# The first convolution group's sums in two attention tiles instead of the fourth raw buffer, and transposes a step or two later

## The chip, the cores and the metric

The kernel runs on one core of a Trainium2 chip. The metric is the device time of one execution in microseconds (us), lower is better. PE is the matrix engine, ACT the scalar engine, DVE the vector engine, SP the engine whose queue issues the loads and most stores.

## The reference

One encoder layer on 256 tokens with 4096 channels. The stream is normalised, projected by one 4096 x 13312 matrix, and split into a convolution branch and an attention branch.

```python
h = layer_norm(x, emb_ln_g, emb_ln_b)
p = h @ w_in                       # c_b, c_c, c_h, c_z, a_q, a_k, a_v, a_z
y_conv = c_b * centred_short_conv(c_c * c_h, conv_w) * silu(c_z)
y_attn = banded_window_attention(a_q, a_k, a_v, sink) * silu(a_z)
y = concat([y_conv, y_attn]) @ w_out
out = layer_norm(2 ** 0.25 * h + y, ln_g, ln_b)
```

All arrays are float32. The convolution is over three neighbouring tokens.

## The kernel before

**Chunks and steps.** The input projection is cut into 26 chunks of 512 columns: K, V, then for each of four attention groups the gate chunk AZ and the query chunk Q, then for each of four convolution groups the chunks CC, CH, CZ, CB. A chunk is a list of steps, 302 in all. A step of kind "in" loads 1 MB of weights and makes 24 matmuls of 512 columns; "half" loads 512 KB and makes 12; "pair" loads 512 KB, forms sums of weight blocks on DVE (a seven-product scheme for a 2 x 2 block product) and makes 21 matmuls of 256 columns. From the fourth chunk on, all have the same twelve steps: in, pair, pair, half, pair, in, pair, pair, in, pair, pair, in. Below, offset n is the step n places behind the first of its chunk (0 to 11).

**The split.** Weights are float32 and the matmul takes a reduced type, so each raw piece is split into a high part (`split_hi`, ACT, L200, tile `whi`) and the rest (`split_lo`, DVE, L204, tile `wlo`). Both are made three steps ahead, and each has three buffers, so the high part of step j+3 can be written only when step j's matmuls are done.

**The raw buffers.** Raw pieces lie in `w0`, `w1`, `w2` and, while the list `extra` names them, in further ones: `w6` of the pool `pw`, later `w7` and `w8` of the pool `pc`. `loads(j)` gives the next piece the buffer whose last piece is oldest. With three buffers it may take the one whose piece is split in the current step (j+3), with more only one whose piece was split a step earlier:

```python
            if u > j + (2 if len(bs) > N_W else 3):
                break
```

All these loads stand in SP's queue in program order, so a load that waits for its buffer holds up those behind it, and stores as well.

**The order in a step.** The order on each engine is the program's: matmuls of step j, `split_hi(j + 3)`, the functions that `at(j, ...)` entered for this step, `loads(j)`, `sums(j + 4)` (L181 to L183, pairs only), `split_lo(j + 3)`. The functions in `later` are the rest of the layer: a chunk's pair products are joined (`pair_copy`, then `pair_sums` a step later), the chunk is completed five steps after its last pair (`whole`, L677), and heads are spread over some 30 steps by `SPREAD` (`scores`, `s_add`, `p_tr`, `p_lo`, `pv`, `out_z`).

**Memory around the change.** Attention tiles lie in the pool `pa`, among them one tile `z` and one tile `q` of 128 x 1024, and `zT`, whose products `out_z` stores to DRAM (`yd`). When attention is over, `open_pc` closes `pa` and opens `pc` in its place, with the convolution's tiles `tm`, `ug`, `t0`, `t1`, the buffers `w7`, `w8` and `yl`. The first convolution group's chunks CC and CH are computed while the last heads are still running, before `pc` exists. Their sums go side by side into the tile in `w6`, which is why `w6` leaves `extra` 18 steps before the chunk CZ of that group begins. That beginning is step `z0` = 134. `product` multiplies the one by the other in place (L682, at z0 + 6), `conv_tr` transposes the product on PE and scales it into `t` on ACT (L696, at z0 + 8 and + 9), `conv_mul` adds the two neighbours on DVE (L702, L704, at z0 + 9 and + 10). `open_pc` stands at z0 + 8. In the later groups, and for the gate chunk CB (`product`, `gate_tr`, `gate_mul`), the same functions stand in the chunk that follows: `product` at offset 4, the transposes at 5 and 6, the rest at 7 and 9.

For the gate chunk AZ, `z_act` applies the SiLU on ACT (L524) at offset 5 of the next chunk, and `z_tr` transposes the result on PE (L481) and copies it to `zT` (L529) at offsets 11 and 13, in the first group at 6 and 7. Transposes, scores and the products with V share two PSUM banks (`att`).

Of the kernel before, what the change touches and what calls it, by code (L numbers as in the profile page):

```python
# [8 lines left out]
F32 = mybir.dt.float32  # L9
F32R = mybir.dt.float32r  # L10
AF = mybir.ActivationFunctionType
ALU = mybir.AluOpType
AX = mybir.AxisListType

P = 128
# [17 lines left out]
W = 512  # L33
# [65 lines left out]
def encoder_kernel(ctx: ExitStack, tc: tile.TileContext, x, emb_g, emb_b, wi, ws, conv_w, sink, wo, ln_g, ln_b, out):  # L99
    nc = tc.nc  # L100
# [57 lines left out]
    def loads(j):  # L158

        nonlocal nxt  # L160
        while nxt < len(steps) and nxt <= j + 7:
            (u, _), bs = w_bufs(nxt)
            if u > j + (2 if len(bs) > N_W else 3):
                break
            load(nxt)
            nxt += 1
# [31 lines left out]
    def split_hi(j):  # L198
        wh[j] = half_tile(j, "whi")
        nc.scalar.activation(part(j, wh[j]), part(j, raw[j]), AF.Copy)  # L200

    def split_lo(j):
        wl[j] = half_tile(j, "wlo")
        nc.vector.tensor_tensor(part(j, wl[j]), part(j, raw[j]), part(j, wh[j]).bitcast(F32), op=ALU.subtract)  # L204
        raw.pop(j)
# [22 lines left out]
    def mm(j):  # L228
        _, ci, q = steps[j]
        hi, lo = wh.pop(j), wl.pop(j)  # L230
        first = j == 0 or steps[j - 1][1] != ci
        last = j == N_IN - 1 or steps[j + 1][1] != ci
        pk, k0 = (2, 2 * q) if steps[j][0] == "half" else (PK, q * PK)
        for k in range(pk):
            kt = k0 + k
            for i in range(2):
                if first and k == 0:
                    acc[ci, i] = ps_acc.tile([P, W], F32, name="acc")
                a = acc[ci, i]
                xh, xl = xT[:, kt, i * P:(i + 1) * P], xT[:, kt, S + i * P:S + (i + 1) * P]  # L240
                hk, lk = hi[:, k * W:(k + 1) * W], lo[:, k * W:(k + 1) * W]
                nc.tensor.matmul(a, xh, hk, start=(first and k == 0), stop=False)  # L242
                nc.tensor.matmul(a, xh, lk, start=False, stop=False)  # L243
                nc.tensor.matmul(a, xl, hk, start=False, stop=(last and k == PK - 1))  # L244
# [3 lines left out]
    def mm_pair(j):  # L248


        _, ci, p = steps[j]
        hi, lo = (t.pop(j).rearrange("p (b w) -> p b w", w=HW) for t in (wh, wl))
        last = p == npairs(ci) - 1
        if p == 0:
            for k in range(2):
                pacc[ci, k] = ps_p.tile([P, 2, HW], F32, name="pacc")
        a, b = 2 * p, 2 * p + 1
        x = lambda kt, i: (xT[:, kt, i * HT:(i + 1) * HT], xT[:, kt, (2 + i) * HT:(3 + i) * HT])
        sc = lambda n: (SC[p][:, 0, n, :], SC[p][:, 1, n, :])
        p0, p1, c0, c1 = pacc[ci, 0], pacc[ci, 1], acc[ci, 0], acc[ci, 1]  # L260
        for (ah, al), w, o, opens, closes in (
                (x(a, 0), 2, p0[:, 0, :], True, False), (x(b, 0), 3, c0[:, 0:HW], False, False),
                (sc(2), 1, c0[:, HW:W], False, False), (x(b, 1), 7, c1[:, 0:HW], False, False),
                (sc(0), 5, p1[:, 1, :], True, False), (x(a, 1) if ci < OUT else sc(3), 6, p0[:, 1, :], False, True),
                (sc(1), 4, p1[:, 0, :], False, True)):
            nc.tensor.matmul(o, ah, hi[:, w, :], start=(opens and p == 0), stop=False)  # L266
            nc.tensor.matmul(o, ah, lo[:, w, :], start=False, stop=False)  # L267
            nc.tensor.matmul(o, al, hi[:, w, :], start=False, stop=(closes and last))  # L268
# [186 lines left out]
    pw = phs.enter_context(tc.tile_pool(name="pw", bufs=1))  # L455
    extra.append((pw, "w6"))
    pa = ph.enter_context(tc.tile_pool(name="pa", bufs=1))
# [30 lines left out]
    st_ = {}  # L488
# [140 lines left out]
    def x_sums(p, t):  # L629

        x = xT[:, 2 * p:2 * p + 2, :]
        xf = t[:, 0:2 * S].rearrange("p (k t) -> p k t", k=2)
        nc.vector.tensor_tensor(xf, x[:, :, 0:S].bitcast(F32), x[:, :, S:2 * S].bitcast(F32), op=ALU.add)
        a11, a12, a21, a22 = (xf[:, k, i * HT:(i + 1) * HT] for i in range(2) for k in range(2))
        s = t[:, 2 * S:4 * S].rearrange("p (k t) -> p k t", k=4)
        for k, o0, o1, op in ((0, a21, a22, ALU.subtract), (3, s[:, 0, :], a11, ALU.subtract),
                              (1, a11, a21, ALU.subtract), (2, a12, s[:, 3, :], ALU.add)):
            nc.vector.tensor_tensor(s[:, k, :], o0, o1, op=op)
        if SC[p].shape[2] == 4:
            return halves(SC[p][:, 0, :, :], SC[p][:, 1, :, :], s)  # L640
        halves(SC[p][:, 0, :, :], SC[p][:, 1, :, :], s[:, 0:3, :])
        halves(x[:, 0, HT:2 * HT], x[:, 0, 3 * HT:4 * HT], s[:, 3, :])

    def sum_tile(ci):

        if ci >= OUT:
            return R[:, :, (ci - OUT) * W:(ci - OUT + 1) * W]
        kind = IN_ORDER[ci]
        if kind >= C_AZ:
            return pa.tile([P, 2, W], F32, name="z")  # L650
        if kind >= C_Q:
            return pa.tile([P, 2, W], F32, name="q")
        name = "ug" if kind < C_CC or C_CH <= kind < C_CZ else "tm"
        if pc is not None:
            return pc.tile([P, 2, W], F32, name=name)
        if name == "tm":
            st_["cu"] = pw.tile([P, 2, 2, W], F32, name="w6", bufs=1)
        return st_["cu"][:, 1 if name == "ug" else 0, :, :]

    def pair_copy(ci):  # L660
        e = st_["e", ci] = sum_tile(ci)
        nc.scalar.activation(e[:, 0, 0:HW], pacc[ci, 0][:, 0, :], AF.Copy)
# [15 lines left out]
        return t  # L678

    def product(key, other):  # L680
        u = st_[key]
        nc.vector.tensor_tensor(u, u, st_[other], op=ALU.mult)  # L682

    def end_cc(ci, c):
        st_["c"] = whole(ci)
# [61 lines left out]
    def at(j, fn, *a):  # L747
        later.setdefault(j, []).append((fn, a))
# [4 lines left out]
    def chunk_end(j, ci):  # L753
        c0, fn = next((c, f) for c, f in ENDS if IN_ORDER[ci] >= c)
        g = IN_ORDER[ci] - c0
        fn(ci, g)
        if fn is end_k:
            at(j + 1, k_turn, g)
        if fn is end_cz:
            at(j + 4, s_act)  # L760
        if fn is end_z:
            at(j + 5, z_act)
            for b in range(2):
                at(j + 11 + 2 * b, z_tr, g, b) if g else at(j + 6 + b, z_tr, g, b)
        if fn is end_q:
            h = g * GROUP
            for t, f, a in SPREAD:
                at(j + t, f, a if f in (q_tr, q_lo) else h + a)
            if g < 2:
                at(j + 22, k_load, g)  # L770
                at(j + 32, v_load, g)
        if fn in (end_ch, end_cb):
            key, other, tr, mul = ("u", "c", conv_tr, conv_mul) if fn is end_ch else ("g", "s", gate_tr, gate_mul)
            last = ci == len(IN_ORDER) - 1
            if last:
                product(key, other)
            else:
                at(j + (6 if ci == c_ch0 else 4), product, key, other)
            for t, f, b in ((2, tr, 0), (2, tr, 1), (3, mul, 0), (3, mul, 1)) if last else (
                    (8, tr, 0), (9, tr, 1), (9, mul, 0), (10, mul, 1)) if ci == c_ch0 else (  # L780
                            (5, tr, 0), (6, tr, 1), (7, mul, 0), (9, mul, 1)):
                at(j + t, f, g, b)

    c_ch0 = IN_ORDER.index(C_CH)
# [7 lines left out]
    z0 = next(j for j, u in enumerate(steps) if u[1] == c_ch0 + 1)  # L792
    for j in range(n_pro, N_IN):
        kind, ci, q = steps[j]
        if j == z0 - 18:
            extra.clear()
        if j == z0 + 10:
            extra.insert(0, (pw, "w6"))
        mm_pair(j) if kind == "pair" else mm(j)
        split_hi(j + 3)  # L800
        for fn, a in later.pop(j, []):
            fn(*a)
        if kind == "pair" and q == PAIRS[ci] - 1:
            pair_copy(ci)
            at(j + 1, pair_sums, ci)
        if j in X_SUMS:
            x_sums(X_SUMS.index(j), pa.tile([P, 4 * S], F32, name="xs", tag="zT", bufs=2))
        if steps[j + 1][1] != ci or j == N_IN - 1:
            if ci == c_ch0:
                at(j + 9, open_pc)  # L810
            if PAIRS[ci]:
                at(j + (4 if j < N_IN - 1 else 1), chunk_end, j + 1, ci)
            else:
                chunk_end(j, ci)
        loads(j)
        sums(j + 4)
        split_lo(j + 3)
# [180 lines left out]
    for n, (c0, w, pk, j0) in enumerate(chunks):  # L998
        us = out_units(n)
        np_ = sum(u[0] == "opair" for u in us)  # L1000
        for t, (kind, _, q) in enumerate(us):
            j = j0 + t
# [118 lines left out]
```

## Time and profile before

| | |
|---|---|
| time, median of 3 runs | 1547.57 us (1547.43 to 1549.18) |
| time of the profiled execution | 1548.43 us |
| its span, first to last instruction | 1546.7 us |
| PE busy | 1524.0 us, 99% |
| DVE busy | 1319.0 us, 85% |
| ACT busy | 777.6 us, 50% |
| DMA | 315.65 MB, mean 204 GB/s |
| TensorE clock granted | 1.00 of full speed |

A matmul's shown duration covers its pipeline; successive matmuls overlap, so PE's busy share is not the share of its peak. In a row of a group stand the count, the busy time, the mean duration in ns, and the idle time of the engine just before the group's instructions with what ended it. In a row of waits stand who waited, for whom, the sum in us, the number of times and the longest. In a row of the timeline stand the start and the duration in us, and in brackets the idle time before it and what ended that. The chain of waits follows the work that ended last back to its causes. SPq is SP's queue of DMA issues.

### The profile page before, as it was taken

The numbers are of one execution on the slowest core, as the hardware profiler recorded it, in microseconds if no ns is written. First come the engines' busy times: TensorE is split into PE (matmuls) and PEld (weight loads), VectorE is DVE, ScalarE is ACT, GpSimd is POOL, SyncE is SP. The second block draws the span as 40 slices with busy tenths as digits, with TensorE's granted clock in tenths as the row PEclk, the third lists the DMA queues.
The fourth block names the chain that finished last, engine by engine and source line by source line (L and its number), as shares of the span: only waits on it lengthen the run. The fifth ranks groups of instructions, "written<-read, shape, count | busy, mean of one in ns | idle before, by whom it ended". The sixth has DMA issues, their size and how long they took to land.

```text
span 1546.7 us, 21715 instructions
## 1 busy us (share of the span) xinstructions
PE 1524.0 (99%) x8843; PEld 1330.5 (86%) x8843; DVE 1319.0 (85%) x1535; ACT 777.6 (50%) x666; POOL 1.3 (0%) x7
## 2 busy tenths in 40 slices
PE   7999999999999999999999999999999999999998
PEld 4888889988988988788888888888888888888897
DVE  7769799899899898988898989998898688888656
ACT  5544546656565554544455455545555444443331
POOL 0000000000000000000000000000000000000000
PEclk9999999999999999999999999999999999999999
DMA  7545554555655545655555555556557756656654
GB/s 290 201 177 196 199 198 162 204 181 191 208 190 171 170 171 201 227 192 210 199 191 204 194 210 196 191 190 229 197 201 274 275 185 226 250 204 225 261 180 141
DMA packets 71428, 315.65 MB, mean 204 GB/s; under 512 B 8512, under 2 KB 12576, under 8 KB 50336
## 3 DMA queue, kind: packets, MB, share of 16 engines
q1 hardware_dynamic: 70320, 312.43, 56.7%
q10 hardware_dynamic: 1008, 1.84, 0.3%
q8 instruction: 69, 1.13, 0.3%
q14 instruction: 31, 0.25, 0.0%
HBM read 305.23 MB, written 8.91 MB: 203 GB/s over the span
## 4 chain that ended last, share of the span: by engine, by line
PE 84%; DVE 11%; DMA 2%; ACT 1%; issue 1%; SPq 0%; ACTq 0%; DVEq 0%
PE acc L242 12%; PE acc L243 12%; PE acc L244 12%; PE acc L908 6%; PE acc L910 6%; PE acc L909 6%; DVE wlo L204 5%; PE pacc L267 4%; PE pacc L266 4%; PE pacc L268 4%; PE acc L266 3%; PE acc L267 3%; PE acc L268 3%; DMA w<-in_ws 2%; DVE w L181 1%; ACT whi L200 1%
## 5 line engine op out<-in xcount | busy, mean ns | idle before, releaser
L200 ACT ACTIVATE whi<-w 128x2048 fp32r<-128x2048 f32 (+1 forms) x352 | 618.1, 1757 | 638.9 <-DVE w L183 209.2
L204 DVE TENSOR_TENSOR wlo<-w,whi 128x2048 fp32r<-128x2048 f32 (+1 forms) x352 | 733.0, 2085 | 147.2 <-ACT whi L200 146.8
L242 PE MATMUL acc<-whi,xT 128*128 128x512 f32 x988 | 390.8, 395 | 0.0
L243 PE MATMUL acc<-wlo,xT 128*128 128x512 f32 x988 | 387.9, 393 | 1.7 <-DVE wlo L204 1.7
L244 PE MATMUL acc<-whi,xT 128*128 128x512 f32 x988 | 387.5, 392 | 0.0
L244 PEld LDWEIGHTS acc<-whi,xT 128*128 128x128 f32 x988 | 185.8, 188 | 41.6
L243 PEld LDWEIGHTS acc<-wlo,xT 128*128 128x128 f32 x988 | 185.8, 188 | 40.8 <-DVE wlo L204 3.8
L242 PEld LDWEIGHTS acc<-whi,xT 128*128 128x128 f32 x988 | 185.8, 188 | 36.3
L908 PE MATMUL acc<-whi,xT 128*128 128x512 f32 (+1 forms) x496 | 182.8, 369 | 0.0
L910 PE MATMUL acc<-whi,xT 128*128 128x512 f32 (+1 forms) x496 | 181.7, 366 | 0.0
L909 PE MATMUL acc<-wlo,xT 128*128 128x512 f32 (+1 forms) x496 | 180.7, 364 | 0.5 <-DVE wlo L204 0.5
L181 DVE TENSOR_TENSOR w<-w 128x512 f32<-128x512 f32 x175 | 119.6, 683 | 8.9 <-DMA w<-in_ws 8.9
L910 PEld LDWEIGHTS acc<-whi,xT 128*128 128x128 f32 x496 | 93.1, 188 | 16.8
L909 PEld LDWEIGHTS acc<-wlo,xT 128*128 128x128 f32 x496 | 93.1, 188 | 16.1 <-DVE wlo L204 0.8
L908 PEld LDWEIGHTS acc<-whi,xT 128*128 128x128 f32 x496 | 93.2, 188 | 14.4 <-issue 0.4
L267 PE MATMUL acc<-wlo,xT 128*128 128x256 f32 x362 | 101.1, 279 | 0.0
L266 PE MATMUL acc<-whi,xT 128*128 128x256 f32 x362 | 101.0, 279 | 0.0
L268 PE MATMUL acc<-whi,xT 128*128 128x256 f32 x362 | 100.9, 279 | 0.0
L266 PE MATMUL pacc<-whi,xT 128*128 128x256 f32 x346 | 98.9, 286 | 0.1
L267 PE MATMUL pacc<-wlo,xT 128*128 128x256 f32 x346 | 96.8, 280 | 0.5 <-DVE wlo L204 0.5
L268 PE MATMUL pacc<-whi,xT 128*128 128x256 f32 x346 | 96.5, 279 | 0.0
L267 PE MATMUL pacc<-wlo,SC 128*128 128x256 f32 x330 | 93.1, 282 | 0.0
(236 smaller groups left out, 2019.1 us busy)
## 6 DMA issues: line engine op xcount, KB each, us to landing
w<-in_wi SPq DMA_DIRECT2D x112, 1024.0 KB
w<-in_ws SPq DMA_DIRECT2D x198, 512.0 KB
w<-in_wo SPq DMA_DIRECT2D x43, 1024.0 KB
R<-in_wo SPq DMA_DIRECT2D x13, 1024.0 KB
x<-in_x SPq DMA_DIRECT2D x7, 512.0 KB
yl<-yd SPq DMA_DIRECT2D x7, 512.0 KB
xc<-in_x SPq DMA_DIRECT2D x14, 256.0 KB
R<-in_ws SPq DMA_DIRECT2D x6, 512.0 KB
```

The costliest lines, as they stand in the source:

```text
L181: nc.vector.tensor_tensor(s01, b22, b12.to_broadcast([P, 2, HW]), op=ALU.add)
L200: nc.scalar.activation(part(j, wh[j]), part(j, raw[j]), AF.Copy)
L204: nc.vector.tensor_tensor(part(j, wl[j]), part(j, raw[j]), part(j, wh[j]).bitcast(F32), op=ALU.subtract)
L242: nc.tensor.matmul(a, xh, hk, start=(first and k == 0), stop=False)
L243: nc.tensor.matmul(a, xh, lk, start=False, stop=False)
L244: nc.tensor.matmul(a, xl, hk, start=False, stop=(last and k == PK - 1))
L266: nc.tensor.matmul(o, ah, hi[:, w, :], start=(opens and p == 0), stop=False)
L267: nc.tensor.matmul(o, ah, lo[:, w, :], start=False, stop=False)
L268: nc.tensor.matmul(o, al, hi[:, w, :], start=False, stop=(closes and last))
L908: nc.tensor.matmul(o, yh, hk, start=first, stop=False)
L909: nc.tensor.matmul(o, yh, lk, start=False, stop=False)
L910: nc.tensor.matmul(o, yl, hk, start=False, stop=last)
```

## The change

- `sum_tile`: while `pc` is not open, the sums of CC go to tile `z` and those of CH to tile `q`, both of `pa`.
- `product`: while `pc` is not open, the result goes to a new tile in `w6` (one half of it is used), no longer over its own operand. It moves from z0 + 6 to z0 + 8.
- `w6` stays a raw buffer until z0 + 4 (before: z0 - 18) and comes back at z0 + 12 (before: z0 + 10).
- `open_pc` moves from z0 + 8 to z0 + 9.
- In the first convolution group `conv_tr` moves from z0 + 8 and + 9 to + 10 and + 11, `conv_mul` from + 9 and + 10 to + 18 and + 21.
- In the other groups `conv_tr`, and in all groups but the last `gate_tr` (the same transposes for the chunk CB), move from offsets 5 and 6 to 6 and 7; their `product` (offset 4) and `conv_mul` or `gate_mul` (7 and 9) stay.
- `z_tr` of the first attention group moves from offsets 6 and 7 to 8 and 9.

```diff
-        if name == "tm":
-            st_["cu"] = pw.tile([P, 2, 2, W], F32, name="w6", bufs=1)
-        return st_["cu"][:, 1 if name == "ug" else 0, :, :]
+        return pa.tile([P, 2, W], F32, name="q" if name == "ug" else "z")
...
     def product(key, other):
-        u = st_[key]
-        nc.vector.tensor_tensor(u, u, st_[other], op=ALU.mult)
+        u, o = st_[key], st_[other]
+        if pc is None:
+            st_[key] = pw.tile([P, 2, 2, W], F32, name="w6", bufs=1)[:, 0, :, :]
+        nc.vector.tensor_tensor(st_[key], u, o, op=ALU.mult)
...
-                at(j + 11 + 2 * b, z_tr, g, b) if g else at(j + 6 + b, z_tr, g, b)
+                at(j + 11 + 2 * b, z_tr, g, b) if g else at(j + 8 + b, z_tr, g, b)
...
-                at(j + (6 if ci == c_ch0 else 4), product, key, other)
+                at(j + (8 if ci == c_ch0 else 4), product, key, other)
...
-                    (8, tr, 0), (9, tr, 1), (9, mul, 0), (10, mul, 1)) if ci == c_ch0 else (
-                            (5, tr, 0), (6, tr, 1), (7, mul, 0), (9, mul, 1)):
+                    (10, tr, 0), (11, tr, 1), (18, mul, 0), (21, mul, 1)) if ci == c_ch0 else (
+                            (6, tr, 0), (7, tr, 1), (7, mul, 0), (9, mul, 1)):
...
-        if j == z0 - 18:
+        if j == z0 + 4:
             extra.clear()
-        if j == z0 + 10:
+        if j == z0 + 12:
             extra.insert(0, (pw, "w6"))
...
-                at(j + 9, open_pc)
+                at(j + 10, open_pc)
```

## The prediction

> **What bounds the kernel now.** I read the busy shares first, then PE's waits over the whole span, then the same waits by stage, and last the chain of waits where PE waits.
>
> ```profile
> PE 1524.0 (99%) x8843; PEld 1330.5 (86%) x8843; DVE 1319.0 (85%) x1535; ACT 777.6 (50%) x666; POOL 1.3 (0%) x7
> ```
>
> PE sets the time: with 99% busy only its waits can be won, as the change leaves the number of matmuls as it is. The view of PE's waits names them:
>
> ```profile
> PE att L382 <- DMA x<-in_x: 8.9, 1, 8.9
> PE att L481 <- ACT z L524: 2.0, 1, 2.0
> PE att L592 <- DVE s L558: 1.8, 1, 1.8
> PE acc L243 <- DVE wlo L204: 1.7, 3, 0.9
> PE att L607 <- DVE pT L599: 1.6, 2, 1.1
> PE att L481 <- DVE ug L682: 1.0, 5, 0.2
> PE pacc L267 <- DVE wlo L204: 0.5, 1, 0.5
> PE att L481 <- issue: 0.3, 1, 0.3
> ```
>
> The first is the start and stays. All others lie where the diff works. Asked for 530 to 660 us alone, the view gives L592, L243, L607 and L267 unchanged, so these seven waits lie there. The busy times by stage say the same (columns: stretch and its length, then PE, PEld, DVE, ACT and POOL busy, the granted clock, the DMA share, GB/s):
>
> ```profile
> 200.00:300.00 100.00, 100.00 (x621) 89.69 (x620) 91.38 (x114) 60.60 (x67) 0.00 (x0) 1.00 0.56 193
> 400.00:490.00 90.00, 90.00 (x573) 81.18 (x572) 81.93 (x105) 54.95 (x64) 0.00 (x0) 1.00 0.56 191
> 540.00:560.00 20.00, 18.21 (x114) 16.08 (x114) 18.43 (x22) 9.65 (x10) 0.00 (x0) 1.00 0.49 179
> 600.00:660.00 60.00, 57.25 (x349) 49.84 (x348) 51.98 (x60) 30.52 (x24) 0.00 (x0) 1.00 0.62 220
> ```
>
> With four raw buffers and the same heads running (200 to 490 us) PE never waits, though DVE is 91% busy. It waits once `w6` has left the raw buffers.
>
> What a wait costs is more than its idle time. Four matmuls in the timeline:
>
> ```profile
> 639.07 0.40 PE L242 MATMUL acc<-whi,xT 128*128 128x512 f32 x1
> 640.33 0.50 PE L243 MATMUL acc<-wlo,xT 128*128 128x512 f32 x1 [0.87 <-DVE wlo L204]
> 640.67 0.39 PE L244 MATMUL acc<-whi,xT 128*128 128x512 f32 x1
> 640.90 0.39 PE L242 MATMUL acc<-whi,xT 128*128 128x512 f32 x1
> ```
>
> Unhindered, as the last two, matmuls of 512 columns start 0.23 us apart though each is shown 0.39 long. The second starts 1.26 us behind the first: 1.03 lost, 0.87 of it shown idle. Every wait therefore costs its idle time plus 0.16 us. The Trainium skill, Perfetto Trace Analysis, section "Summary: the profiler window per engine type", says that a TensorE row ends at an estimated end; the trace agrees, with 0.39 against 0.23. Counting shown idle time alone, as if rows did not overlap, the waits below would sum to 8.9 in place of 11.1 us and the forecast would be 1539.2.
>
> **The change part by part.**
>
> **1. `w6` a raw buffer for 22 steps longer.** In the stretch 520 to 660 us DVE waits for loads, and from 600 on ACT once for a store:
>
> ```profile
> DVE w L181 <- DMA w<-in_ws: 3.9, 5, 1.2
> ACT t L696 <- DMA yd<-zT: 3.4, 1, 3.4
> ```
>
> The chain of waits shows the loop behind the first:
>
> ```profile
> 540.83 2.28 DVE wlo L204
> 546.43 1.95 DVE wlo L204
> 548.39 3.10 DMA w<-in_ws
> 551.59 0.70 DVE w L181
> ```
>
> The load of piece 131 waits for `split_lo` of 128, which frees its buffer (548.38), lands 3.1 us later, and DVE's sums wait for it; that is the longest of the five, 1.2 us. With the fourth buffer the same load takes the buffer of 127, free when the `wlo` of 540.83 ends (543.11): 5.3 us earlier against 1.2 missing. DVE, never late for a load, then runs as it does from 400 to 490. The waits L592 (once) and L607 (twice), both for DVE functions of heads queued behind the late sums, go: 1.8 + 1.6 + 3 x 0.16 = 3.9 us. By the rule of `loads`, pieces 123 to 144 are each loaded a split earlier; only 145 to 148 keep the three-buffer rule, since `w6` leaves at z0 + 4 and `w7` comes at z0 + 9. Behind the split that frees the buffer for 148, DVE has another split of 2.3 us (like that of 540.83) and three sums before it comes to the sums of 148, about the 3.1 us of a landing. I take 0 for these four loads, and the longest wait, 1.2 us, as the upper bound.
>
> **2. The product at z0 + 8.** One DVE instruction as before, of the same size; writing elsewhere adds no instruction. Its place is the step of offset 8, after `out_z`, where DVE one group of chunks earlier had nothing to do:
>
> ```profile
> L682 DVE TENSOR_TENSOR w<-w x1: 1210/1210/1210, 603.7 to 603.7; 128x1024 f32<-128x1024 f32 x1
> 513.02 0.42 DVE L612 TENSOR_TENSOR zT<-att,zT 128x256 f32<-128x256 f32 x1
> 515.81 2.29 DVE L204 TENSOR_TENSOR wlo<-w,whi 128x2048 fp32r<-128x2048 f32 x1 [2.37 <-ACT whi L200]
> ```
>
> 1.2 us fit into 2.4 idle: cost 0, and the place at z0 + 6 is relieved. If that cover were gone, at most 1.2. The new waits, of `pair_copy` for the tiles `z` and `q`, end early: their last readers on PE are done nine and twelve steps before.
>
> **3. The pool and the group's transposes and multiplications later.** Before, the store of the last head held up both ACT and SP's queue:
>
> ```profile
> 610.77 0.42 SPq L613 DMA_DIRECT2D yd<-zT  x1
> 615.58 1.29 SPq L156 DMA_DIRECT2D w<-in_ws  x3
> 615.62 0.84 ACT L696 ACTIVATE t<-att,cw 128x256 f32<-128x256 f32 x2 [3.43 <-DMA yd<-zT]
> L702 DVE SCALAR_TENSOR_TENSOR t<-att,cw,t x16: 473/475/483, 616.5 to 1134.5; 128x255 f32<-128x255 f32 x16
> L704 DVE SCALAR_TENSOR_TENSOR t<-att,cw,t x16: 482/483/485, 617.0 to 1135.1; 128x255 f32<-128x255 f32 x16
> ```
>
> The pool's first use must wait for the store's landing, 4.8 us after its issue. ACT stood 3.4 us in front of `conv_tr`'s scaling with the next `split_hi` behind it; then 2 x 4 instructions of 0.48 us, 3.8 in all, pushed DVE's splits back, and PE met four late `wlo` (L243 three times, L267 once). In the new order two more pair steps (21 matmuls at 0.12 us, 2.5 us each, the spacing of the first rows in part 4) and four transposes lie between the end of the step of `out_z` and the scaling, 5.4 us against the 4.8, and `out_z` runs about at that end (513.02 in the chunk above): ACT waits a little at most. SP meets the pool one step later, behind a load that has to wait for a split in any case. The four waits go: 1.7 + 0.5 + 4 x 0.16 = 2.8 us.
>
> The multiplications, 1.9 us each, go to offsets 6 and 9 of the chunk CB. What they meet at offset 6 is shown by a chunk without such work there:
>
> ```profile
> 738.45 4.02 DVE L204 TENSOR_TENSOR wlo<-w,whi 128x1792 fp32r<-128x1792 f32 x2
> 742.58 0.28 PE L266 MATMUL pacc<-whi,xT 128*128 128x256 f32 x1
> ```
>
> The first of the two splits ends at 740.47, and the matmuls of its step begin at 742.58: 2.1 us spare, 1.9 used. At offset 9 later groups multiply already, without a wait of PE on `wlo` in the view above. Cost 0, the upper bound 1.9 each, by a margin of 0.2. They hold both `att` banks from z0 + 10 to + 21, and no other function needs one then: the heads end at z0 + 8, `gate_tr` begins at z0 + 30.
>
> **4. `z_tr` of the first group two steps later.**
>
> ```profile
> 178.79 0.28 PE L267 MATMUL pacc<-wlo,SC 128*128 128x256 f32 x1
> 178.91 0.28 PE L268 MATMUL pacc<-whi,SC 128*128 128x256 f32 x1
> 181.15 0.66 PE L481 MATMUL att<-ident,z 128*128 128x128 f32 x4 [1.96 <-ACT z L524]
> 180.04 1.06 ACT L524 ACTIVATE z<-z 128x1024 f32<-128x1024 f32 x1
> 179.15 2.28 DVE L204 TENSOR_TENSOR wlo<-w,whi 128x2048 fp32r<-128x2048 f32 x1
> ```
>
> The transposes wait for a SiLU that ends at 181.10. Two steps later PE reaches them after another pair step and 24 wide matmuls, 5.5 us at least: no wait, 2.0 + 0.16 = 2.1 us gained. Next late is the `wlo` of step 34, done at 181.43: without the stall and without the transposes PE starts that step at 181.5 (21 matmuls at 0.12 us after 179.03), so it just holds. If it did not, some tenths would come back.
>
> **5. Transposes of the other groups a step later.** Six times they came right behind the product (L481 for `ug`, five times, and "issue" once): 1.0 + 0.3 + 6 x 0.16 = 2.3 us. A pair step now lies between. `conv_mul` keeps its step, and its scaled tile is there a step later; DVE gets to it only after two more splits. Next late is the split for offset 8:
>
> ```profile
> 777.87 2.28 DVE L204 TENSOR_TENSOR wlo<-w,whi 128x2048 fp32r<-128x2048 f32 x1
> 780.44 0.40 PE L242 MATMUL acc<-whi,xT 128*128 128x512 f32 x1
> ```
>
> It ends at 780.15. PE, 0.36 earlier, would start the step at 780.08 and need it 0.23 later, at 780.31. That leaves 0.16 us; the cost lies between 0 and all of the 2.3. I take 0.
>
> **The sum.** 3.9 + 2.8 + 2.1 + 2.3 = 11.1 us, of which I leave 0.5 for margins of 0.2 and less that fail here and there: 10.6. The profiled execution took 1548.43 us, which gives 1537.8; the median of the runs is 0.86 lower, which gives 1537.0.
>
> **The rivals.**
>
> *The second cluster only moves.* The 3.8 us of multiplications stall the splits of the chunk CB, or the pool's store still holds ACT. For it: a margin of 0.2 at offset 6. Against: at offset 9 the same work is done without loss. Gain 10.6 - 2.8 = 7.8: 1539.8. Its rule in the Trainium skill is in DMA: Bandwidth & Descriptors, section "Anatomy of one DMA — SWDGE (gpsimd) path": a DMA's end is signalled only when its last byte is confirmed, worst for a store to device memory, with some 2 us fixed. By its fit a 128 KB store takes an estimated 2.3 us. The trace has 4.8 from issue to the next load. By 2.3 the pool would explain only 0.9 of ACT's 3.4 us, a quarter of the 2.8, and the sum would come to some 1539.1; the measured time decides.
>
> *Loads are late by rate, not by buffers.* Then the first cluster stays: 10.6 - 3.9 = 6.7, 1540.9. Against it: no such wait of DVE at 400 to 490 us with the same traffic (191 GB/s there, 179 at 540).
>
> *The transposes' 2.3 us come back as waits for `wlo`* at offset 8, by the margin of 0.16: 8.3, 1539.3. The same for part 4: 1539.1.
>
> *Slower.* SP's queue is in order. If the first load into the new pool waits much longer than the 4.8 us, all weights behind it wait. PE pays nothing until the pieces in hand are used, among them two steps of 5.5 us before piece 149 is split; to undo the gain the wait would have to exceed 11 by another 10.6 us, some 22 us. At 25 us the time would be 1551.0. Nothing in the trace is near that.
>
> *Nothing happens:* the waits have causes that I do not see, and less than 3 us go: about 1546.
>
> **How the numbers follow.** Forecast 0.56, second cluster 0.13, rate 0.08, transposes or `z_tr` back 0.17, nothing 0.04, slower 0.02. 0.2%, 3.1 us, is about what a measurement of this kernel can tell from no change. Every case but the last two is faster by more: 0.94, with 0.04 and 0.02. Range: 1536.0 (all 11.1, and half a microsecond of the runs' spread) to 1541.0, which takes in each rival on the faster side; two of them together lie beyond.
>
> **What would show it.** PE's waits: the rows of L592, L607, L267, of L481 for z and for ug gone, L243 near nothing. DVE's row for loads into `w` in 520 to 660 us at most 1.2. ACT's row for yd gone. PE busy equal to the stage's length from 540 to 650. The prediction is wrong if new rows of `wlo` L204 stand among PE's waits near 183 us, near offset 8 of the chunks after CH and CB, or in the chunk of the moved multiplications.

## The result and the profile after

The changed kernel takes 1536.72 us in the median of 4 runs (1536.44 to 1537.77), the kernel before 1547.5 us (1546.91 to 1549.18): 10.8 us less, a ratio of 0.993 with a 95% interval of 0.9913 to 0.9947. 1537.0 us had been forecast. The profiled execution took 1536.44 us with a span of 1534.7 us.

The page and the view of PE's waits over the whole span, after:

```profile
span 1534.7 us, 21713 instructions
PE 1520.8 (99%) x8843; PEld 1330.3 (87%) x8843; DVE 1318.3 (86%) x1535; ACT 777.6 (51%) x666; POOL 1.3 (0%) x7
PE att L382 <- DMA x<-in_x: 8.8, 1, 8.8
PE att L969 <- ACT lhs L951: 0.4, 1, 0.4
PE att L607 <- DVE pT L599: 0.3, 1, 0.3
PE acc L243 <- DVE wlo L204: 0.3, 1, 0.3
PE acc L909 <- DVE wlo L204: 0.2, 1, 0.2
```

Seven rows stood in the place of L607 and L243 before, with 8.9 us in 14 waits. Two waits are left, with 0.6 us. With 0.16 us of lost overlap for each of the 12 that went, that is 8.3 + 1.9 = 10.2 us.

The stages where PE had waited, after (columns as in the prediction):

```profile
540.00:560.00 20.00, 20.00 (x126) 17.93 (x125) 18.90 (x24) 10.83 (x12) 0.00 (x0) 1.00 0.58 208
600.00:660.00 60.00, 59.67 (x357) 52.81 (x356) 53.45 (x60) 32.04 (x24) 0.00 (x0) 1.00 0.64 229
```

PE is busy all of the first stage (18.21 of 20 before), and in it DVE has as much work as ever. DVE's wait for loads between 510 and 660 us, and the scaling on ACT that stood 3.4 us for the store:

```profile
DVE w L181 <- DMA w<-in_ws: 1.2, 1, 1.2
612.76 0.82 ACT L696 ACTIVATE t<-att,cw 128x256 f32<-128x256 f32 x2
```

Five waits for loads became one, and no idle time stands before the scaling.

The spans differ by 12.0 us, more than the waits account for. A second measure needs no rule for lost overlap: each matmul of one trace is set against the same one of the other, and the change in the distance of their starts is the time lost or won between two places. A figure found so is called matched below. Matched, the changed kernel is 0.2 us behind from the start and 10.7 us ahead at 1400 us. The other 1.3 us come in the last part of the kernel, where the same matmuls were issued a little faster in this execution; the section on the hardware shows that this goes by the execution and not by the kernel.

### The profile page after: what moved, and what is told of

It is laid out like the page before. It is cut to its first block, busy times and chain, and to the rows that moved or that the text cites. A ratio compares the mean times of both kernels' runs of the same rounds, so it can differ in the third digit from the quotient of the medians.

```text
span 1534.7 us, 21713 instructions
## 1 busy us (share of the span) xinstructions
PE 1520.8 (99%) x8843; PEld 1330.3 (87%) x8843; DVE 1318.3 (86%) x1535; ACT 777.6 (51%) x666; POOL 1.3 (0%) x7
## 4 chain that ended last, share of the span: by engine, by line
PE 97%; DVE 1%; DMA 1%; ACT 0%; SPq 0%; issue 0%; ACTq 0%
PE acc L243 15%; PE acc L242 15%; PE acc L244 15%; PE acc L908 6%; PE acc L910 6%; PE acc L909 6%; PE pacc L267 5%; PE pacc L266 5%; PE pacc L268 5%; PE acc L267 4%; PE acc L266 4%; PE acc L268 4%; PE att L481 1%; PE acc L369 1%; DVE wlo L204 1%; DMA w<-in_ws 0%
## 5 line engine op out<-in xcount | busy, mean ns | idle before, releaser
L243 PE MATMUL acc<-wlo,xT 128*128 128x512 f32 x988 | 388.3, 393 | 0.3 <-DVE wlo L204 0.3
L243 PEld LDWEIGHTS acc<-wlo,xT 128*128 128x128 f32 x988 | 185.7, 188 | 39.7 <-DVE wlo L204 2.5
```

## Experiments

All were compared with the kernel before on the chip on which they ran. The medians of one kernel moved by up to 2.5 us between chips and series, so for parts of 1 to 3 us the waits in the traces decide and the times only support them.

### The fourth buffer idle

```diff
-        if j == z0 + 4:
+        if j == z0 - 18:
             extra.clear()
```

> The changed kernel, but the fourth raw buffer leaves the raw buffers at z0 - 18 as before and stays unused until the product. Theory (three buffers make loads late): DVE again waits some 4 us for loads in 520 to 600 us, PE's waits for the heads (L592, L607) come back, 3.9 us: about 0.9975 of the changed kernel, span near 1538.5. Rival (loads are late by the rate of the DMA, and what helped is the rest): no such waits, span stays at 1534.7 within 1 us.

Median 1540.55 us, ratio 0.9944 (0.9928 to 0.9961), span 1539.6. PE's waits between 530 and 660 us, DVE's wait for loads between 510 and 660, and one stage:

```profile
PE att L592 <- DVE s L558: 1.8, 1, 1.8
PE att L607 <- DVE pT L599: 0.9, 2, 0.5
PE acc L243 <- DVE wlo L204: 0.3, 1, 0.3
DVE w L181 <- DMA w<-in_ws: 4.6, 4, 1.7
550.00:560.00 10.00, 8.16 (x40) 6.85 (x40) 9.76 (x14) 5.17 (x8) 0.00 (x0) 0.83 0.47 153
```

The waits for loads are back, and with them the waits for the heads: against the changed kernel 1.8 + 0.6 + 2 x 0.16 = 2.7 us of PE. The rate is refuted: the same pieces over the same queue, only one buffer less. It is 2.7 and not 3.9 because the later waits of L607 come back only in part. The span is longer by 4.9. Another 1.6 us of that come from the granted clock, which fell to 0.83 in the stage shown, where eight matmuls came 0.43 us apart in place of 0.23; no other run has that there. The rest lies outside this stretch.

### The second cluster: pool and multiplications, each alone and both

Three kernels place the pieces of the first group as before, each time with the fourth buffer in use. Pool early, multiplications late:

```diff
-                at(j + (8 if ci == c_ch0 else 4), product, key, other)
+                at(j + (6 if ci == c_ch0 else 4), product, key, other)
-                    (10, tr, 0), (11, tr, 1), (18, mul, 0), (21, mul, 1)) if ci == c_ch0 else (
+                    (8, tr, 0), (9, tr, 1), (18, mul, 0), (21, mul, 1)) if ci == c_ch0 else (
-        if j == z0 + 12:
+        if j == z0 + 10:
-                at(j + 10, open_pc)
+                at(j + 9, open_pc)
```

> The changed kernel, but product, pool and transposes of the first group stand two steps (the pool one step) earlier, as in the kernel before; the multiplications stay late and the fourth buffer stays in use. Theory: ACT again waits 3 to 3.5 us for the last head's store, but the next split has about as much to spare, so PE loses 0 to 0.5 us, span 1534.7 to 1535.2. Rival (ACT's wait is what carries the second cluster): 2 to 2.8 us more, span 1536.7 to 1537.5, with waits of L243 for the split behind the wait.

Median 1536.55 us, ratio 0.9923 (0.9908 to 0.9938), span 1534.8. ACT's wait between 585 and 660 us, then PE's between 530 and 660:

```profile
ACT t L696 <- DMA yd<-zT: 3.6, 1, 3.6
PE att L607 <- DVE pT L599: 0.3, 1, 0.3
PE acc L243 <- DVE wlo L204: 0.3, 1, 0.3
```

ACT waits 3.6 us for the store as it did before, and PE's two waits are those of the changed kernel. The pool's wait by itself makes no wait of PE (matched up to 660 us, PE falls 0.2 us behind).

Multiplications early, pool late:

```diff
-                    (10, tr, 0), (11, tr, 1), (18, mul, 0), (21, mul, 1)) if ci == c_ch0 else (
+                    (10, tr, 0), (11, tr, 1), (11, mul, 0), (12, mul, 1)) if ci == c_ch0 else (
```

> The changed kernel, but the first group's two multiplications stand one step behind their transposes again (z0 + 11 and z0 + 12 in place of z0 + 18 and z0 + 21); the pool still opens late. Theory (the pool's wait and the 3.8 us of multiplications cost the 2.8 us of the second cluster together, and DVE has most of the room that the multiplications need once it is on time): 0.3 to 1.0 us more, span 1535.0 to 1535.7. Rival (the multiplications alone make the second cluster): 2.8 us more, span 1537.5.

Median 1539.21 us, ratio 0.9938 (0.9924 to 0.9953), span 1537.5. PE's waits between 530 and 660 us, and DVE's timeline around the multiplications:

```profile
PE acc L243 <- DVE wlo L204: 1.9, 3, 0.9
PE att L607 <- DVE pT L599: 0.3, 1, 0.3
...
617.25 0.47 DVE L702 SCALAR_TENSOR_TENSOR t<-att,cw,t 128x255 f32<-128x255 f32 x1
619.07 0.41 DVE L667 TENSOR_TENSOR tm<-tm,pacc 128x256 f32<-128x256 f32 x1
620.78 2.02 DVE L204 TENSOR_TENSOR wlo<-w,whi 128x1792 fp32r<-128x1792 f32 x1
622.71 0.48 DVE L702 SCALAR_TENSOR_TENSOR t<-att,cw,t 128x255 f32<-128x255 f32 x1
626.05 1.22 DVE L204 TENSOR_TENSOR wlo<-w,whi 128x1024 fp32r<-128x1024 f32 x1
```

1.6 us more in two more waits, 1.9 us of PE (matched: 2.2). I had expected at most 1.0. Between the two blocks of 1.9 us (from 617.25 and 622.71) stand the four instructions of `pair_sums` (from 619.07, 1.7 us) and a split, and DVE is busy without a gap until the split of step 149 ends at 627.27. The expectation had set the multiplications against what the splits had to spare and left out `pair_sums` between them. That is read from the timeline; no run moved `pair_sums` alone.

Both early, with the pool: the diff of the first kernel, with (9, mul, 0), (10, mul, 1).

> The changed kernel, but product, pool, transposes and multiplications of the first group all stand where they stood before; only the fourth buffer and the two sum tiles are new in this group. Theory (pool and multiplications make the second cluster together): 2 to 2.8 us more, span 1536.7 to 1537.5, with three or four waits for the split between 605 and 650 us. Rival (the second cluster was an echo of the first: DVE was already late by some us when it began): the cluster stays away, at most 1 us more.

Median 1539.9 us, ratio 0.9943 (0.9929 to 0.9958), span 1538.6. PE's waits between 530 and 660 us, ACT's between 585 and 660, and one of DVE's between 510 and 660:

```profile
PE acc L243 <- DVE wlo L204: 1.7, 3, 0.9
PE pacc L267 <- DVE wlo L204: 0.5, 1, 0.5
PE att L607 <- DVE pT L599: 0.4, 1, 0.4
ACT t L696 <- DMA yd<-zT: 3.4, 1, 3.4
DVE t L702 <- ACT t L696: 2.0, 1, 2.0
```

For splits 1.9 us more idle in three more waits, 2.4 us (matched: 3.2): the second cluster is back, so it was no echo of the first. Of the 2.4, the multiplications carry 1.9 alone (matched: 2.2), and the pool's wait adds 0.5 (matched: 1.0). The last row shows how it adds: a multiplication that stands one step behind the transposes needs the tile that ACT scales late, and DVE waits 2.0 us for it, as in the kernel before. Neither of the other two kernels has that row.

### The fourth buffer alone

The kernel before, with only the two sum tiles, the product into `w6`, and `w6` a raw buffer until z0 + 4.

```diff
-        if j == z0 - 18:
+        if j == z0 + 4:
             extra.clear()
```

> The kernel before with one part of the change alone: the sums of the first group lie in the tiles z and q, the product goes to the fourth buffer, which stays a raw buffer until z0 + 4; everything else stands where it stood. Theory (the parts add up): the waits for the heads shrink from 3.9 to 0.5 us, the waits of the second cluster (2.8), of z (2.1) and of ug (2.3) stay: 3.4 us faster than before, span 1543.3. Rival (the fourth buffer does most of it, since a DVE that is on time also shrinks the second cluster): 5 us or more, span below 1541.7.

Median 1545.79 us of 11 runs against 1547.95, ratio 0.9979 (0.997 to 0.9988), span 1544.3. PE's waits between 530 and 660 us:

```profile
PE acc L243 <- DVE wlo L204: 1.6, 3, 0.9
PE pacc L267 <- DVE wlo L204: 0.5, 1, 0.5
PE att L607 <- DVE pT L599: 0.4, 1, 0.4
```

L592 is gone and L607 down from 1.6 to 0.4: 1.8 + 1.2 + 2 x 0.16 = 3.3 us, as expected, and the ratio's interval holds 1.9 to 4.6 us (the medians differ by 2.2). Matched against the kernel before up to 610 us, 3.4 us are won. The second cluster stands as before. The parts add up.

### The product early

```diff
-                at(j + (8 if ci == c_ch0 else 4), product, key, other)
+                at(j + (6 if ci == c_ch0 else 4), product, key, other)
```

> The changed kernel, but the first group's product stands at z0 + 6 again, before the heads' last functions on DVE are done. Theory: 1.2 us of DVE in front of the sums of piece 144 and the split of 143, which have 2.8 us to spare: 0 to 0.3 us more, span 1534.7 to 1535.0. Rival (the place of the product is part of the gain): 1.2 us more, span 1535.9.

Median 1535.68 us, ratio 0.9907 (0.9892 to 0.9922), span 1533.3. PE's waits between 530 and 660 us:

```profile
PE att L607 <- DVE pT L599: 0.4, 1, 0.4
PE acc L243 <- DVE wlo L204: 0.3, 1, 0.3
```

The same two waits as in the changed kernel. Where the product stands matters to nothing. The span's 1.4 us are not its doing: 0.7 of them are there at 204 us, where the two programs are still the same.

### The gate's transposes back

```diff
-                at(j + 11 + 2 * b, z_tr, g, b) if g else at(j + 8 + b, z_tr, g, b)
+                at(j + 11 + 2 * b, z_tr, g, b) if g else at(j + 6 + b, z_tr, g, b)
```

> The changed kernel, but the first gate chunk's transposes stand at offsets 6 and 7 again. Theory: PE waits 2.0 us for the SiLU at about 181 us, 2.1 us in all, and nothing of it comes back later: span 1536.8. Rival (what the stall cost is made up for by later waits that it spares): less than 1 us more.

Median 1539.81 us, ratio 0.9935 (0.9917 to 0.9952), span 1536.8. PE's waits hold one row more than in the changed kernel:

```profile
PE att L481 <- ACT z L524: 2.0, 1, 2.0
```

The span grows by the expected 2.1 us, but by luck. Matched, this execution was 0.5 us ahead from the start; it then lost 2.0 us by the stall and 1.5 us by a drop of the granted clock right behind it (shown in the section on the hardware), and gained 0.9 us in stretches up to 1200 us where the changed kernel's execution was issued more slowly. The stall is better read elsewhere. In the prediction's lines of the kernel before, the transposes start 2.24 us behind the last matmul in place of 0.12: 2.1 us. The kernel with the fourth buffer alone has the same stall without a drop of the clock: there PE falls 1.9 us behind the changed kernel at it and is still 1.7 us behind at 530 us, so hardly anything is made up for.

### The other groups' transposes back

```diff
-                            (6, tr, 0), (7, tr, 1), (7, mul, 0), (9, mul, 1)):
+                            (5, tr, 0), (6, tr, 1), (7, mul, 0), (9, mul, 1)):
```

> The changed kernel, but the transposes of the other groups stand at offsets 5 and 6 again. Theory: six waits of 0.2 to 0.25 us behind the product are back, 0.36 each with the lost overlap, 2.3 us: span 1537.0. Rival (the part of a wait that is no idle time is no loss): 1.3 us more, span 1536.0.

Median 1540.85 us, ratio 0.994 (0.9922 to 0.9958), span 1539.5. The added rows among PE's waits that lie in the stage of these transposes:

```profile
PE att L481 <- DVE ug L682: 1.0, 5, 0.2
PE att L481 <- PE acc L244: 0.4, 1, 0.4
```

1.4 us of idle time in six waits, with the overlap 2.4 us, as expected by the theory. Matched against the changed kernel, PE falls behind by 2.5 us within some 10 us of the six waits, well over the idle time alone. Up to 1130 us it is 3.2 us: behind three of the waits the matmuls also came a little slower for some 30 us, 0.233 us apart in place of 0.229. The span's 4.8 us hold another 2.1 us from after 1420 us, where the matmuls of this execution were issued more slowly, less 0.5 us that the changed kernel's execution lost around 1170 us.

### The two waits that are left

The split that PE waits for at 643 us in the changed kernel starts on ACT behind this (ACT's timeline, changed kernel):

```profile
636.64 1.28 ACT L711 ACT_TABLE_LOAD   x1
637.94 1.06 ACT L711 ACTIVATE tm<-tm 128x1024 f32<-128x1024 f32 x1
638.90 3.49 ACT L200 ACTIVATE whi<-w 128x2048 fp32r<-128x2048 f32 x2
```

The kernel before has the same table load and, behind it, the same wait of PE:

```profile
644.88 1.28 ACT L711 ACT_TABLE_LOAD   x1
651.42 0.50 PE L243 MATMUL acc<-wlo,xT 128*128 128x512 f32 x1 [0.37 <-DVE wlo L204]
```

So this is one of the three L243 waits of the kernel before, and not a new one. First the SiLU alone was moved:

```diff
-            at(j + 4, s_act)
+            at(j + (5 if g == 0 else 4), s_act)
```

> The changed kernel, but the first convolution group's SiLU stands one step later (offset 5 of the next chunk in place of 4). In the changed kernel PE has one wait for a split left there, 0.33 us shown at 643.2 (0.5 with the lost overlap), and the split's first half on ACT starts right behind a table load of 1.28 us and the SiLU of 1.06. Theory (that split waits for ACT): the wait goes, 0.5 us less, span 1534.2. Rival (DVE's late multiplications make it): the wait stays, span 1534.7.

Median 1536.13 us, ratio 0.9911 (0.9896 to 0.9926), span 1534.2. Between 530 and 660 us PE has one wait left, and no row for the split:

```profile
PE att L607 <- DVE pT L599: 0.4, 1, 0.4
```

So the split waited for ACT. Then the other one as well:

```diff
-                at(j + t, f, a if f in (q_tr, q_lo) else h + a)
+                at(j + t - (g == 3 and f is p_lo and a == 2), f, a if f in (q_tr, q_lo) else h + a)
```

> The changed kernel with the two waits of PE that are left in the stage taken away: the first convolution group's SiLU one step later, and in the last attention group the third head's low part (p_lo) one step earlier, ahead of the split and the sums that it waited behind. Theory: 0.5 us for each, 1.0 us less than the changed kernel, no wait of PE between 30 and 1400 us. Rival (the earlier p_lo pushes the split of step 139, which has 1.7 us to spare, and the sums behind it, so that a wait for the split comes instead): 0.5 us less, with a new row for wlo.

> The changed kernel once more, as the partner on the same chip of the next one: 10.6 to 12 us faster than before.

On one chip the changed kernel took 1536.07 us (ratio 0.9918, 0.9904 to 0.9931) and this one 1535.61 us (0.9913, 0.9899 to 0.9926). PE's waits over its whole span:

```profile
PE att L382 <- DMA x<-in_x: 8.8, 1, 8.8
PE att L969 <- ACT lhs L951: 0.4, 1, 0.4
PE acc L909 <- DVE wlo L204: 0.4, 1, 0.4
```

Between the start and the last part of the output projection no wait is left that the view lists, and no new one for a split. The medians differ by 0.5 us in the right direction, but the intervals overlap: shown in the trace, not in the time.

## Why the prediction was right

**The sum.** 11.1 us of waits with 0.5 left over gave 10.6; the medians give 10.8. What stayed was 1.0 us (two waits of 0.33 and 0.35, each with 0.16) in place of 0.5. Two small waits, at 543.17 and 627.77 us with 0.02 and 0.06 us of idle time shown, went with the others and had not been counted; matched, each cost 0.3. That the two errors nearly cancel is luck.

**Lost overlap.** That a wait costs more than it shows idle held; that it is 0.16 us more each time did not. The 0.16 was read from one start. In the same four matmuls of the prediction the next start is late too, 0.34 us behind in place of 0.23, so that this wait cost 1.14 us, 0.27 over its idle time. Matched wait by wait, the addition is some 0.1 us for the waits of the heads, 0.16 for the gate's stall, 0.2 behind the product and 0.2 to 0.3 for waits on a split. The mean was near enough for the sum: by idle time alone the forecast would have been 1539.2, outside the runs of the changed kernel.

**Part 1** held in its mechanism, and in its size to some tenths: 3.3 us with the fourth buffer alone and 2.7 lost again with it idle, where 3.9 had been forecast. Load 148, taken at 0, made DVE wait 1.2 us and PE not at all; that 1.2 was also the bound is a coincidence, as the bound was another load's wait. One head's wait (L607) remained at 0.3, which the analogy with the earlier chunks had not shown.

**Part 2** held: cost 0 at either place. That z0 + 6 is "relieved" was worth nothing.

**Part 3** came near in its size and was wrong in part of its cause. Of the four waits that it counted, three went: 1.8 us idle and 2.3 by the prediction's rule, 3.2 matched, where 2.8 had been forecast. The fourth, 0.37 us at 651.42 before and 0.33 at 643.18 after, had been put down to the multiplications. It comes from the SiLU and its table load on ACT, which the prediction had not looked at. For the other three, the chain "ACT stood 3.4 us, then the multiplications pushed DVE's splits back" gave both a share in series. The runs show that ACT's wait alone costs next to nothing, that the multiplications alone cost 1.9, and that ACT's wait adds to them where a multiplication has to wait for ACT's tile. What made the change worth its while here is that the 3.8 us of DVE work left a place where, by the timeline, `pair_sums` and the splits already filled DVE. The margin of 0.2 at offset 6 was enough: no new wait for a split stands in that chunk.

**Parts 4 and 5** held: 2.1 and 2.4 us, against 2.1 and 2.3, each undone by itself. Part 5 won another 0.7 us in the slower stretches behind the waits, which the prediction had not counted.

**The rivals.** The rate of the loads is refuted by the idle buffer. The second cluster did not move. The transposes' waits did not come back as waits for `wlo` at offset 8; the split with 0.16 us to spare is nowhere among the waits. The queue of SP held nothing up that reached PE. The Trainium skill, DMA: Bandwidth & Descriptors, section "Anatomy of one DMA — SWDGE (gpsimd) path", would have had the store land in an estimated 2.3 us and the pool explain a quarter of the second cluster. Its fit is for the gpsimd path, while this store went by SP's queue, and the trace has 4.8 us. The share came out near a quarter all the same, 0.5 of 2.4 (matched: 1.0 of 3.2), but for another reason: ACT did wait 3.4 to 3.6 us for the store, and that reached DVE only through the early multiplications.

## What to carry to other kernels

Where PE is 99% busy, list its few waits, add to each the overlap that it breaks (read at every late start behind it, not only the first), and follow each back to the engine that is late. Here such a sum came within a few tenths of 10.8 us of 1547, with some luck. A wait seen upstream, like ACT's 3.4 us for a store, costs next to nothing until the engine below it has to wait for it and has no room, so before moving it, count everything else that the late engine does between the two points. Margins of an engine at 90% were well read from a place in the same trace with the same pattern, and should be read for every engine that feeds the split, not only for the one whose work was moved.

## What was not expected of the hardware

In the last part of the output projection the same matmuls of 256 columns were issued at one of two rates, by the execution. Three rows of the stages, PE alone (length, PE busy with the count, granted clock, DMA share, GB/s): first the changed kernel, then the same kernel in its second series, then the kernel with the other groups' transposes back.

```profile
1492.00:1507.00 15.00, 15.00 (x134) 1.00 0.52 177
1492.00:1507.00 15.00, 15.00 (x129) 1.00 0.43 147
1492.00:1507.00 15.00, 15.00 (x129) 1.00 0.75 253
```

134 or 129 matmuls in 15 us, 0.112 or 0.116 us each, with a granted clock of 1.00 and PE never idle in all three. The slower rate began at different times and cost up to 2.1 us of a span. It is as large as the parts told apart here and shows as no wait, so spans of single executions were compared only with it in mind. What sets it was not found.

The granted clock was not steady either. In two of the traces it stood at half for 3.4 us in mid-execution, right behind one of PE's longest waits. Rows as above, first the kernel with the fourth buffer idle, behind a wait of 1.8 us, then the one with the gate's transposes back, behind a wait of 2.0 us:

```profile
554.80:558.10 3.30, 3.30 (x9) 0.50 0.71 288
181.70:185.00 3.30, 3.30 (x18) 0.50 0.91 295
```

Each drop cost some 1.5 us on top of the wait. The kernel before has both waits, and the kernel with the fourth buffer alone has the second; no drop followed in their traces, so it comes in some executions and not in others. Over all timed executions with a recorded clock, a mean of 0.998 stands in 13 of the 48 of these four kernels and in none of the 36 of the others, where no wait of this length is left. On one chip the kernel before took 1550.0 us in the median with that mean and 1547.6 us with 1.00. So taking away a wait of 2 us may win more than the wait. That the lower means are such drops is likely but not shown, since only the profiled executions have a trace.
